# A one-layer streaming-encoder trunk on one core: a conditioning row loaded once and spread by products with ones, and the short chunks of the second feed-forward product put first

## The chip, the cores and the metric

The kernel runs on one core of one Trainium2 chip. The metric is device time in microseconds (us) of one execution; lower is better. The time before the change is the median of three executions, 2311.63 us (2308.95 to 2312.49).

## What is computed

One layer, 512 tokens, width 2048, feed-forward width 5632, all in 32-bit floats. A conditioning vector `c` sets six modulation vectors; two head groups of eight heads each (a gated linear recurrence and a stick-breaking attention) share one input projection; a gated residual, a second modulated normalisation and a SwiGLU feed-forward net follow.

```python
cond = jax.nn.silu(c)                                    # c: (1, 2048)
mod = cond @ w_ada + b_ada                               # 6 x 2048
sh1, sc1, g1, sh2, sc2, g2 = split(mod, 6)
h = rms_norm(x, norm1_g) * (1.0 + sc1) + sh1
proj = h @ w_in
o = concat(hgrn2_mixer(proj[...]), stick_breaking_mixer(proj[...]))
x = x + g1 * (o @ w_out)
h = rms_norm(x, norm2_g) * (1.0 + sc2) + sh2
gate, up = split(h @ w_ffn_in, 2)                        # 5632 each
x = x + g2 * ((silu(gate) * up) @ w_ffn_out)
```

The change touches two ends of this: how `silu(c)` comes to stand in all 128 partitions, and the order in which the 44 blocks of 128 feed-forward rows go through the last product.

## The kernel before

Everything is written with a tile framework: the code names tiles and pools, and a list scheduler sets the order in which the instructions stand on each engine, from the order in the code, from priorities (`tc.high_priority`) and from its own estimate of when each operand is ready. Each engine then runs its own list strictly in that order. All loads and stores are issued by SyncE (SP), whose list is in order too; eight completion semaphores go round, so the ninth load waits until the first has landed.

Products run with both operands split in a rounded part and a rest (`split`, lines 212 to 222: ScalarE copies the rounded part, line 220, VectorE subtracts, line 221). Three matmuls of 512 columns then make one product of two tiles (high by high, high by rest, rest by high). Four buffers go round for the rounded parts, so a copy on ScalarE waits until TensorE has finished with the part split four places earlier.

**The start of the program** (lines 270 to 324, tile `st` in the profile). The host lays `c` out 128 times, so that `a["c"]` has 128 rows of 2048 numbers, 1 MB. Lines 274 to 278 load it in two halves, and the first modulation row of the weights `w_ada` (`ada_first`) in two halves between them; ScalarE applies silu to each half of `cond`. A modulation number is the sum along a row of `w_ada` times `cond`, one VectorE instruction with an accumulator (`gemv`, line 180). From the first two sums come `mod` (line 293) and `gain` (line 184), and with the gain ScalarE makes the first scaled and rounded tile of x, `hhi` (line 309), which the first matmul waits for; VectorE makes the rest, `hlo` (line 310). Between them stand the load of ScalarE's second activation table (line 279), a short exponential for the head groups (line 592), the split of the first weight tile `wi0` in two halves (lines 298 and 299), and the squares of x (lines 312 and 315). Then 16 steps of 24 matmuls follow, each with a row of `w_ada`, a weight tile and a block of x loaded for it.

**The second feed-forward product** (lines 1163 to 1283, tiles `foA`, `foB`, `foC`). A one-level Strassen scheme with seven products makes out of 44 blocks of 128 rows, paired into 22, and 512 tokens the 2048 output columns. The 22 pairs go in six chunks, `CHUNKS = (4, 4, 4, 4, 3, 3)`; each chunk is done for two column groups, which makes 12 units. In a unit the seven products stand in the order `ORDER`; a product of a chunk of n pairs is 6n matmuls, so a unit is 168 matmuls with n = 4 and 126 with n = 3. `multiply` (line 1174) splits the weights of a product two pairs at a time (instructions on 1024 columns; a third pair alone makes one of 512), and before it VectorE makes the Strassen sums of the weights (lines 1181 and 1245). `onto` (line 1193) takes a finished product out of PSUM: in the first chunk ScalarE copies it to the output tile `O` (line 1196), in later chunks ScalarE copies it to a quarter of `cond` (line 1201) and VectorE adds it (line 1202); two products per unit are added from PSUM directly (lines 1259 and 1266). This part of a unit does not depend on n. In the last chunk the finished output blocks are transposed by TensorE (tile `foB` with `ident`), scaled and added to the residual by VectorE (line 1213) and stored (line 1215), as far as they are ready, three after each product.

The left operands of the second product are made in the first one: `keep` (line 1056) turns each pair of finished feed-forward blocks into seven forms, splits them and stores them in DRAM tiles `opd`, one for each chunk (`parts`, line 1076, ScalarE's cast on line 1082, VectorE's on 1083); `load_op` (line 1018) brings them back into a ring of eleven places, a chunk ahead. For the last pair, at line 1081, the rounded parts go to the tile `cond`. Its sums and casts stand, by the schedule, in the middle of the first unit of the second product.

Of the kernel before, what the change touches and what calls it, by code (L numbers as in the profile page):

```python
# [14 lines left out]
AF = mybir.ActivationFunctionType  # L15
# [5 lines left out]
T = 512  # L21
# [2 lines left out]
FM = 44  # L24
HT = 256
HALF = 8
CHUNKS = (4, 4, 4, 4, 3, 3)
ORDER = (2, 1, 7, 6, 4, 5, 3)
AHEAD = 300
SC2_EARLY = 8  # L30
# [99 lines left out]
def trunk(ctx, tc, a):  # L130
    nc = tc.nc
    V, S, G = nc.vector, nc.scalar, nc.gpsimd
    clock = Clock()
    PE = Timed(nc.tensor, clock)
# [9 lines left out]
    def acc(name):  # L144
        return psum.tile([P, T], F32, tag="acc", name=name)

    def att(name):
        return psum.tile([P, T], F32, tag="att", name=name, bufs=2)
# [4 lines left out]
    cond = const.tile([P, D], F32, name="cond")  # L153
    small = const.tile([P, N_SMALL], F32, name="small")
    ones = const.tile([P, P], F32, name="ones")
# [15 lines left out]
    def raw_tile(shape, name):  # L171
        return wp.tile(shape, F32, tag="raw", name=name, bufs=4)
# [97 lines left out]
    banks = [acc(f"st{i}") for i in range(4)] + [att(f"st{i + 4}") for i in range(2)]  # L270
    wide = att2("st6")
    banks += [wide[:, 0:T], wide[:, T:2 * T]]
    r0 = raw_tile([P, D], "ada_first")
    for i in range(2):
        sl = slice(i * 1024, i * 1024 + 1024)
        nc.sync.dma_start(cond[:, sl], a["c"][:, sl])
        nc.sync.dma_start(r0[:, sl], a["w_ada"][SC1 * KT][:, sl])
        S.activation(cond[:, sl], cond[:, sl], AF.Silu)
    tc.keep_in_program_order(S.preload_act_table_set("natural_log_exp_and_others"))
    nc.sync.dma_start(small, a["small"])  # L280
    w0 = raw_tile([P, 1024], "wi0r")
# [4 lines left out]
    for k in range(KT):  # L286
        xk = xo[:, k]
        if k == 0:
            for i in range(2):
                sl = slice(i * 1024, i * 1024 + 1024)  # L290
# [704 lines left out]
    rp = tctx.enter_context(tc.tile_pool(name="rp", bufs=1, side="right", reuse_waits="tile"))  # L995
    opd = [dram.tile([P, 7, n, 2 * HT], F32, name=f"opd{c}") for c, n in enumerate(CHUNKS)]
    starts = [sum(CHUNKS[:c]) for c in range(len(CHUNKS))]

# [11 lines left out]

    units = [(c, i) for c in range(len(CHUNKS)) for i in range(2)]
    places, blocks = [], [{} for _ in units]

    def place(n):
        n %= 11
        return places[0][:, n] if n < 4 else places[1][:, n - 4] if n < 7 else places[2][:, n - 7]

    def load_op(c, q):
        if c < len(CHUNKS):
            nc.sync.dma_start(place(7 * c + q)[:, 0:CHUNKS[c]].bitcast(F32),  # L1020
                              opd[c][:, ORDER[q] - 1].rearrange("p n (h t) -> p n h t", h=2))

    def load_y(u, b):
        if u == len(units):
            return
        c, i = units[u]
        n = CHUNKS[c]
        t = raw_tile([P, n, T], f"wfo{u}_{b}") if b % 2 == 0 else yraw[u > 0][:, b // 2, 0:n]
# [314 lines left out]
```

## Time and profile before

| | |
|---|---|
| median of three executions | 2311.63 us (2308.95 to 2312.49) |
| the profiled execution's own time | 2309.45 us |
| its span, first to last instruction | 2307.6 us |
| granted TensorE clock, mean | 0.995 |
| busy: TensorE matmuls, VectorE, ScalarE | 98%, 83%, 50% |
| DMA rate over the span | 190 GB/s; 368 GB/s in the first fortieth |
| stages by TensorE's tile: first projection `st` | from 11.54 us |
| second feed-forward product `fo` | from 1850.33 us |

The profile is one execution. A row of the timeline gives start, duration, engine, line, operation and operands (out<-in); in square brackets stands the time for which the engine was idle before it and what ended the wait. Matmuls are pipelined: the recorded 0.39 us of one overlaps with the next, and the distance of the starts is what TensorE needs. A row of the windows gives the busy time and number of instructions of each engine in a stretch of time, then the granted TensorE clock (PEclk), the DMA share and rate.

### The profile page before, as it was taken

Reading aid. Unit: us, or ns where it says so; the run is one execution under the profiler, and the core shown is the slowest. Engines: PE = TensorE matmul, PEld = TensorE weight load, DVE = VectorE, ACT = ScalarE, POOL = GpSimd, SP = SyncE. Lnnn points to the kernel's source line nnn. Section 1 sums busy time; section 2 is a strip of 40 time slices with the busy share of each in tenths; the row PEclk is TensorE's granted clock in tenths of the full one; section 3 lists DMA queues with packets and bytes.
Section 4 is the critical chain, followed back from the end, with each engine's and each line's share of the span. In section 5 each row is a group of like instructions: output and inputs, shape, how many; then the busy total and the mean of one; then the engine's idle time right before and its main releaser. Section 6 shows DMA issues by size and latency. Waiting matters only on the chain.

```text
span 2307.6 us, 35720 instructions
## 1 busy us (share of the span) xinstructions
PE 2253.1 (98%) x14171; PEld 2049.8 (89%) x14171; DVE 1919.5 (83%) x2570; ACT 1160.1 (50%) x2011; POOL 10.7 (0%) x25
## 2 busy tenths in 40 slices
PE   8999899999999999989999999999999999999998
PEld 6899799888888788989999999999999978878776
DVE  8887779999887864699899988888888777888888
ACT  4326666565656422654445444454545545454443
POOL 0000000000000000000000000000000000000000
PEclk9999999999999999999999999999999999999999
DMA  9886446843322486336555534454544486654553
GB/s 368 314 319 225 166 153 230 305 170 126 110 92 76 155 294 209 111 114 238 206 203 197 209 133 165 142 174 142 174 142 157 177 343 237 219 178 142 183 204 87
DMA packets 114978, 437.69 MB, mean 190 GB/s; under 512 B 9822, under 2 KB 58236, under 8 KB 76796
## 3 DMA queue, kind: packets, MB, share of 16 engines
q1 hardware_dynamic: 114812, 435.42, 53.0%
q8 instruction: 111, 1.82, 0.3%
q14 instruction: 55, 0.45, 0.1%
HBM read 386.61 MB, written 48.77 MB: 189 GB/s over the span
## 4 chain that ended last, share of the span: by engine, by line
PE 79%; DVE 11%; DMA 4%; ACT 3%; issue 3%; SPq 0%; DVEq 0%; ACTq 0%
PE ffA L93 17%; PE ffC L93 9%; PE foA L93 8%; PE sbp L93 8%; PE wo L93 7%; PE ffB L93 4%; PE foC L93 4%; PE st L93 4%; PE hgf L93 4%; PE hgq L93 3%; PE hgg L93 3%; PE foB L93 1%; DVE ada L180 1%; PE l L93 1%; DMA opd<-fhi 1%
## 5 line engine op out<-in xcount | busy, mean ns | idle before, releaser
L180 DVE SCALAR_TENSOR_TENSOR ada<-ada,cond 128x2048 f32<-128x2048 f32 x95 | 216.9, 2286 | 49.0 <-DMA ada<-in_w_ada 49.0
L93 PE MATMUL ffA<-opD,ff_3h 128*128 128x256 f32 x512 | 93.6, 283 | 0.8 <-ACT u L1008 0.8
L93 PE MATMUL ffA<-opB,ff_6h 128*128 128x256 f32 x512 | 93.6, 283 | 0.2 <-ACT a L1008 0.2
L93 PE MATMUL ffC<-opB,ff_7h 128*128 128x256 f32 x512 | 93.5, 283 | 0.0
L93 PE MATMUL ffC<-opC,ff_4h 128*128 128x256 f32 x496 | 90.8, 284 | 0.4 <-ACT c L1008 0.3
L93 PE MATMUL ffB<-opA,ff_2h 128*128 128x256 f32 x496 | 91.3, 284 | 0.0
L93 PE MATMUL ffA<-opC,ff_5h 128*128 128x256 f32 x496 | 90.6, 283 | 0.0
L93 PE MATMUL ffA<-opA,ff_1h 128*128 128x256 f32 x496 | 90.6, 283 | 0.0
L1082 ACT CAST fhi<-forms 128x512 fp32r<-128x512 f32 (+1 forms) x63 | 43.6, 692 | 90.6 <-DMA opd<-fhi 74.1
L93 PEld LDWEIGHTS ffA<-opD,ff_3h 128*128 128x128 f32 x512 | 79.8, 192 | 1.0 <-ACT u L1008 1.0
L93 PEld LDWEIGHTS ffA<-opB,ff_6h 128*128 128x128 f32 x512 | 79.7, 192 | 0.4 <-ACT a L1008 0.4
L93 PEld LDWEIGHTS ffC<-opB,ff_7h 128*128 128x128 f32 x512 | 79.8, 192 | 0.0
L93 PEld LDWEIGHTS ffC<-opC,ff_4h 128*128 128x128 f32 x496 | 77.2, 192 | 0.8 <-ACT c L1008 0.8
L93 PEld LDWEIGHTS ffB<-opA,ff_2h 128*128 128x128 f32 x496 | 77.7, 193 | 0.1
L93 PEld LDWEIGHTS ffA<-opC,ff_5h 128*128 128x128 f32 x496 | 77.3, 192 | 0.0
L93 PEld LDWEIGHTS ffA<-opA,ff_1h 128*128 128x128 f32 x496 | 77.3, 192 | 0.0
L1083 DVE TENSOR_TENSOR forms<-forms,fhi 128x512 fp32r<-128x512 f32 (+1 forms) x63 | 49.0, 778 | 31.0 <-ACT fhi L1082 30.6
L93 PE MATMUL ffA<-opD,ff_3l 128*128 128x256 f32 x256 | 72.5, 283 | 0.0
L93 PE MATMUL ffC<-opB,ff_7l 128*128 128x256 f32 x256 | 72.4, 283 | 0.0
L93 PE MATMUL ffA<-opB,ff_6l 128*128 128x256 f32 x256 | 72.4, 283 | 0.0
L93 PE MATMUL ffB<-opA,ff_2l 128*128 128x256 f32 x248 | 70.3, 284 | 0.0
L93 PE MATMUL ffA<-opA,ff_1l 128*128 128x256 f32 x248 | 70.2, 283 | 0.0
(1644 smaller groups left out, 7759.3 us busy)
## 6 DMA issues: line engine op xcount, KB each, us to landing
ada<-in_w_ada SPq DMA_DIRECT2D x95, 1024.0 KB, 5.0
wfo<-in_w_fo SPq DMA_DIRECT2D x16, 1024.0 KB, 6.0
yraw<-in_w_fo SPq DMA_DIRECT2D x16, 1024.0 KB, 5.1
fix<-in_w_fix SPq DMA_DIRECT2D x14, 1024.0 KB, 5.7
opsA<-opd SPq DMA_DIRECT2D x12, 1024.0 KB, 4.9
opd<-forms SPq DMA_DIRECT2D x44, 256.0 KB, 3.7
opd<-fhi SPq DMA_DIRECT2D x42, 256.0 KB, 4.2
opd<-forms SPq DMA_DIRECT2D x22, 384.0 KB, 6.7
```

The lines of the kernel that those rows point to most:

```text
L93: self.engine.matmul(out, lhsT, rhs, **kw)
L180: V.scalar_tensor_tensor(w, w, 1.0, row, op0=ALU.mult, op1=ALU.mult, accum_out=col)
L1082: S.copy(hi, R[:, q])
L1083: V.tensor_sub(R[:, q].bitcast(F32R), R[:, q], hi.bitcast(F32))
```

## The change

There are two independent parts. The first loads one row of `c` (8 KB) instead of 128; for each quarter of 512 columns a matmul with a row of ones as the stationary operand copies the row into all 128 partitions of a PSUM tile, and ScalarE applies silu from there into `cond`. The load of the row goes ahead of both halves of `ada_first`. The second part turns the chunk sizes round. Lines after 282 move down by four.

```diff
-CHUNKS = (4, 4, 4, 4, 3, 3)
+CHUNKS = (3, 3, 4, 4, 4, 4)
...
     r0 = raw_tile([P, D], "ada_first")
+    nc.sync.dma_start(cond[0:1], a["c"][0:1])
     for i in range(2):
         sl = slice(i * 1024, i * 1024 + 1024)
-        nc.sync.dma_start(cond[:, sl], a["c"][:, sl])
         nc.sync.dma_start(r0[:, sl], a["w_ada"][SC1 * KT][:, sl])
-        S.activation(cond[:, sl], cond[:, sl], AF.Silu)
+
+    for i in range(4):
+        sl = slice(i * T, i * T + T)
+        PE.matmul(banks[4 + i], ones[0:1], cond[0:1, sl], start=True, stop=True)
+        S.activation(cond[:, sl], banks[4 + i], AF.Silu)
```

The schedule moves with both parts. At the start of the program, on ScalarE, the list before begins like this (`st_...` are PSUM tiles, `wi0` the first weight tile, `xo` blocks of x; in brackets what the instruction waits for, DMAHW being a load):

```order
L278 ACT_TABLE_LOAD
L278 ACTIVATE cond<-cond 128x1024 [waits DMAHW0_49]
L278 ACTIVATE cond<-cond 128x1024 [waits DMAHW2_49]
L279 ACT_TABLE_LOAD
L298 CAST wi0h<-wi0r 128x512 [waits DMAHW5_49]
L592 ACTIVATE lbt<-lbt 128x8 [waits DVE_49]
L309 ACTIVATE hhi<-xo,gain_80 128x512 [waits DMAHW6_49,DVE_49]
```

After the change the same list begins so:

```order
L282 ACT_TABLE_LOAD [waits DMAHW0_49]
L282 ACTIVATE cond<-st_102 128x512 [waits PE_49]
L282 ACTIVATE cond<-st_103 128x512 [waits PE_49]
L302 CAST wi0h<-wi0r 128x512 [waits DMAHW4_49]
L282 ACTIVATE cond<-st_104 128x512 [waits PE_49]
L316 ACTIVATE ss_97<-xo 128x512 [waits DMAHW5_49]
L302 CAST wi0h<-wi0r 128x512 [waits DMAHW6_49]
L319 ACTIVATE sq_174<-xo 128x512 [waits DMAHW7_49]
L282 ACTIVATE cond<-st_104 128x512 [waits PE_49]
L283 ACT_TABLE_LOAD
L596 ACTIVATE lbt<-lbt 128x8 [waits DVE_49]
L313 ACTIVATE hhi<-xo,gain_80 128x512 [waits DVE_49]
```

The third silu has moved behind the cast of the first half of `wi0`, and the fourth behind both casts and the squares of two blocks of x. VectorE's list at the same place reads before:

```order
L180 SCALAR_TENSOR_TENSOR ada_first,lead<-ada_first,cond 128x1024 x2
L517 TENSOR_SCALAR qkg<-small 128x1
L518 COPY qkg<-small 128x1
L293 SCALAR_TENSOR_TENSOR mod<-lead,small 128x1
L591 TENSOR_TENSOR lbt<-small 128x8
L184 SCALAR_TENSOR_TENSOR gain_80<-mod,small 128x1
L299 TENSOR_TENSOR wi0l<-wi0r,wi0h 128x512
L594 RECIPROCAL lbs<-lbt 128x8
L595 TENSOR_TENSOR lbt<-lbt,lbs 128x8
L310 SCALAR_TENSOR_TENSOR hlo<-xo,gain_80,hhi 128x512
```

and after:

```order
L599 TENSOR_TENSOR lbt<-lbt,lbs 128x8
L184 SCALAR_TENSOR_TENSOR gain_80<-mod,small 128x1
L600 TENSOR_TENSOR lbt<-lbt 128x8
L601 TENSOR_SCALAR oml<-lbt 128x8
L180 SCALAR_TENSOR_TENSOR ada_161,mod<-ada_161,cond 128x2048
L314 SCALAR_TENSOR_TENSOR hlo<-xo,gain_80,hhi 128x512
```

These rows come after the two `ada_first` sums, between which now stand the rests of `wi0` and the first sum of squares; the reciprocal of `lbt` stands ahead of `mod` and `gain`, and the first `hlo` stands behind the next row's sum of 2048 columns.

In the first unit of the second product, on ScalarE, the list before is (`wfo_4_2h` is the second split of that unit's fifth product, `forms` holds the last feed-forward pair, `O` the output):

```order
L220 CAST wfo_4_0h<-wfo_2_18705 128x1024 [waits DVE_49,PE_49,Activation_49]
L220 CAST wfo_4_2h<-wfo_2_18705 128x1024 [waits DVE_49,PE_49,Activation_49]
L1082 CAST cond<-forms_18478 128x512 [waits DVE_49]
L1082 CAST cond<-forms_18478 128x768 [waits DVE_49]
L1082 CAST cond<-forms_18478 128x512
L1196 COPY O<-foA_18745 128x512 [waits DMAHW5_49]
L1196 COPY O<-foA_18746 128x512
L1196 COPY O<-foC 128x512 x2
```

After the change it is:

```order
L220 CAST wfo_4_0h<-wfo_2_18710 128x1024 [waits DVE_49,PE_49,Activation_49]
L1086 CAST cond<-forms_18483 128x512 [waits DVE_49]
L220 CAST wfo_4_2h<-wfo_2_18710 128x512 [waits PE_49,Activation_49]
L1086 CAST cond<-forms_18483 128x512 [waits DVE_49]
L1086 CAST cond<-forms_18483 128x768 [waits DVE_49]
L1200 COPY O<-foA_18750 128x512 [waits DMAHW4_49]
L1200 COPY O<-foA_18751 128x512
L1200 COPY O<-foC 128x512 x2
```

One of the three casts of the last pair has moved ahead of the split `wfo_4_2h`, the split has half its columns, and the copies to `O` still stand behind all of them.

On TensorE, in some units the third product (`foC`) begins in the middle of the second (`foA`). Of the units with three pairs the tenth is such a one before the change:

```order
L93 MATMUL foA0_18745<-wfo9_1_2h_21035,opsC_18998 128x512
L93 MATMUL foA0_18745<-wfo9_1_2l_21036,opsC_18998 128x512
L93 MATMUL foA0_18745<-wfo9_1_2h_21035,opsC_18998 128x512
L93 MATMUL foC_18751<-opsB_18715,opsC_18998 128x512 x12
L93 MATMUL foC_18751<-wfo9_2_2h_21068,opsC_18998 128x512
```

After the change it is the fourth unit:

```order
L93 MATMUL foA0_18750<-wfo3_1_2h_19429,opsC_18961 128x512
L93 MATMUL foA0_18750<-wfo3_1_2l_19430,opsC_18961 128x512
L93 MATMUL foA0_18750<-wfo3_1_2h_19429,opsC_18961 128x512
L93 MATMUL foC_18756<-opsB_18720,opsC_18961 128x512 x12
L93 MATMUL foC_18756<-wfo3_2_2h_19462,opsC_18961 128x512
```

What stood in the tenth unit stands in the fourth; in the first three units the second product stands whole, before and after.

## The prediction

> **What bounds the kernel now.** I read the page's first lines, then who TensorE waits for, then the chain that ended last, then the timeline of the two places that the change touches.
>
> ```profile
> span 2307.6 us, 35720 instructions
> PE 2253.1 (98%) x14171; PEld 2049.8 (89%) x14171; DVE 1919.5 (83%) x2570; ACT 1160.1 (50%) x2011; POOL 10.7 (0%) x25
> ```
>
> ```profile
> PE st L93 <- ACT hhi L309: 11.5, 1, 11.5
> PE foA L93 <- ACT O L1196: 3.4, 1, 3.4
> ```
>
> ```profile
> 11.54 88.72 PE st L93 x378
> ```
>
> TensorE is the bound: busy 98% of the span. Its longest waits are the 11.5 us until the first matmul and, third in that view, 3.4 us in the first unit of the second product; the change touches both places. From the first matmul on, the chain runs through TensorE without a break for 88.72 us, so whatever delays that matmul delays all that follows, and what makes a transfer shorter helps only if the first matmul comes sooner. The profiled execution took 2309.45 us, 1.85 around its span and 2.2 under the median of three, 2311.63; I add the changes to the median. A measurement of this kernel can tell about 0.2%, 4.6 us, from no change.
>
> **Part one, the conditioning row.** The start of the program, with the loads' medians below it:
>
> ```profile
> 0.74 0.40 SPq L276 DMA_DIRECT2D cond<-in_c  x1
> 4.64 1.06 ACT L278 ACTIVATE cond<-cond 128x1024 f32<-128x1024 f32 x1 [2.63 <-DMA cond<-in_c]
> 5.97 1.23 DVE L180 SCALAR_TENSOR_TENSOR ada_first<-ada_first,cond 128x1024 f32<-128x1024 f32 x1 [5.97 <-DMA ada_first<-in_w_ada]
> 8.74 1.28 ACT L279 ACT_TABLE_LOAD   x1
> 9.04 1.23 DVE L180 SCALAR_TENSOR_TENSOR ada_first<-ada_first,cond 128x1024 f32<-128x1024 f32 x1 [1.84 <-DMA ada_first<-in_w_ada]
> 10.03 0.62 ACT L298 CAST wi0h<-wi0r 128x512 fp32r<-128x512 f32 x1
> 10.57 0.16 DVE L184 SCALAR_TENSOR_TENSOR gain<-mod,small 128x1 f32<-128x1 f32 x1
> 10.64 0.21 ACT L592 ACTIVATE lbt<-lbt 128x8 f32<-128x8 f32 x1
> 11.54 0.80 PE L93 MATMUL st<-wi0h,hhi 128*128 128x512 f32 x1 [11.54 <-ACT hhi L309]
> 11.61 0.75 DVE L310 SCALAR_TENSOR_TENSOR hlo<-xo,gain,hhi 128x512 fp32r<-128x512 f32 x1
> 11.91 0.60 ACT L298 CAST wi0h<-wi0r 128x512 fp32r<-128x512 f32 x1
> 12.42 0.62 ACT L315 ACTIVATE sq<-xo 128x512 f32<-128x512 f32 x1
> 14.38 2.29 DVE L180 SCALAR_TENSOR_TENSOR ada<-ada,cond 128x2048 f32<-128x2048 f32 x1 [0.54 <-DMA ada<-in_w_ada]
> ```
>
> ```profile
> cond<-in_c SPq DMA_DIRECT2D x2, 512.0 KB, 3.9
> out_y<-O SPq DMA_DIRECT2D x32, 128.0 KB, 1.9
> ```
>
> Now the loads set the pace here: the second sum waits until 9.04 for its weights. Both halves of `cond` gone, what is queued behind them lands up to 3.07 us sooner (9.04 less 5.97, one half of each). That would be a gain, if the order on ScalarE stayed. It doesn't: the fourth silu, without which the second sum can't run, now stands behind two casts and two squares, and ahead of the table load.
>
> The four products with ones come first on TensorE. Their price is that of the one product of this form in the trace, the sum of squares:
>
> ```profile
> 101.97 1.02 PE L93 MATMUL ssum<-ss,ones 128*128 128x512 f32 x2
> 103.00 0.34 PE L93 MATMUL sbp<-wsb_0l,hhi 128*128 128x384 f32 x1
> 103.17 0.34 PE L93 MATMUL sbp<-wsb_0h,hlo 128*128 128x384 f32 x1
> ```
>
> From 101.97 to 103.00 it and one matmul of 384 columns were done; the latter takes 0.17 (103.00 to 103.17), so the product takes 0.86. At the start TensorE is at half pace:
>
> ```profile
> 13.98:17.39 3.41, 3.41 (x10) 1.00 1.04 422
> 17.39:20.80 3.41, 3.41 (x17) 1.00 1.03 405
> 1867.42:1870.83 3.41, 0.56 (x2) 1.00 0.20 67
> 1870.83:1874.24 3.41, 3.41 (x9) 0.50 0.93 308
> ```
>
> In equal stretches there are 10 matmuls before 17.39 us and 17 after it; the column of the granted clock has no record for the start, but at 1870.83, after 2.85 us of idleness in one stretch of 3.41, it says 0.50 for the next, with the same 9 or 10. So a product with ones takes 1.72 at the start.
>
> The sum, from the row's load at 0.74: landed 2.6 (1.9 later, as the 128 KB of `out_y`, the nearest in size; 3.9 as `cond` is the other bound), three products 5.2, so 7.8; the third silu 0.6 (a 512-column activation, as the cast at 10.03), 8.4; squares 0.62, cast 0.60, squares 0.62, 10.2; the fourth silu, 10.8. The loads they need are there: even the second block of x, in place by 12.42 before, has landed by 9.4. The fourth product, which waits for the third silu, is done by 10.1. Then the second sum 1.23 on VectorE, beside the table load 1.28 and the exponential 0.21 on ScalarE, to 12.3; the reciprocal, `mod` and `lbt` ahead of `gain`, about 0.2 each as the rows of this size: `gain` at 12.9. From `gain` to the first matmul 0.97, as now (10.57 to 11.54): 13.87, less about 0.1 for each pair of overlapping ScalarE instructions (11.91 to 12.42 is 0.51 for 0.60): 13.6. That is 2.1 later than 11.54. Then `hlo`, which the sixth matmul needs, stands behind a sum of 2.29: it is done 0.3 + 2.29 + 0.75 after `gain`, near 16.2, while five matmuls at half pace (0.34 apart at 10 in 3.41, up to 0.43 by twice the later pace) end at 15.3 to 15.8: 0.4 to 0.9 of waiting, 0.5 taken. The half pace lasted from 11.54 to 17.39, 5.85; stretches of 3.41 that do not start with the program would make it 3.4 to 6.8, 5.1 on the mean; half of the difference of 0.75 is 0.3 to gain. Sum of part one: **+2.3**. Bounds: if the row lands after 3.9, +4.3; if the first three products run at full pace, the first cast, whose load can land no sooner than about 7.0, takes their place, and I find +1.5. A gain is excluded only as long as ScalarE's order holds.
>
> The Trainium skill, "ScalarE: Activation LUTs", section "What ACT_TABLE_LOAD costs", gives 1.28 us for the load of a table and 1.38 for a drain behind it, 2.66 in all. Here the load of 8.74 is followed by a cast at 10.03, so this trace shows the 1.28 alone; by the page part one would be 1.4 dearer.
>
> **Part two, the short chunks first.** The units of the second product, from first matmul to first matmul (first, second, fourth, and the last four):
>
> ```profile
> 1850.33:1893.79 43.46, 40.03 (x171) 32.60 (x169) 32.07 (x34) 21.36 (x27) 0.00 (x0) 0.96 0.90 356
> 1893.79:1931.87 38.08, 38.08 (x170) 31.53 (x168) 28.46 (x27) 19.79 (x24) 0.00 (x0) 1.00 0.79 303
> 1969.95:2009.59 39.64, 39.00 (x169) 31.30 (x168) 33.17 (x35) 18.73 (x22) 0.00 (x0) 1.00 0.72 265
> 2168.19:2198.87 30.68, 30.24 (x129) 23.61 (x128) 25.70 (x34) 15.21 (x22) 0.00 (x0) 1.00 0.40 129
> 2198.87:2230.89 32.02, 30.10 (x128) 23.33 (x126) 26.78 (x35) 15.08 (x22) 0.00 (x0) 1.00 0.66 228
> 2230.89:2264.42 33.53, 31.73 (x144) 24.74 (x142) 31.32 (x45) 15.24 (x23) 0.00 (x0) 1.00 0.45 147
> 2264.42:2299.15 34.73, 32.97 (x157) 26.04 (x156) 32.45 (x50) 12.91 (x19) 0.00 (x0) 1.00 0.22 61
> ```
>
> The second unit has no stall: 168 matmuls in 38.08, 0.2267 each; 126 would take 28.56. A unit of four pairs once the additions have begun takes 39.64, so it loses 1.56. Those of three pairs lose more, since VectorE is at 26.78 in 32.02 (84%) and taking products out of PSUM costs it the same for a smaller unit: the tenth loses 32.02 - 28.56 = 3.46, the ninth (128 matmuls fall in its stretch, 29.02) 1.66. The last two, with the output's transposes, take 68.26 for 250 matmuls (56.7): 11.6 over. The first loses 5.38: the wait of 3.4 and one stretch of half clock, 1.7. All losses: 5.38 + 5 x 1.56 + 1.66 + 3.46 + 11.6 = 29.9.
>
> After the change the first unit has this to it:
>
> ```profile
> 1864.89 0.68 DVE L1064 TENSOR_TENSOR forms<-sg,up 128x512 f32<-128x512 f32 x1
> 1866.92 1.04 ACT L220 CAST wfo_2h<-wfo 128x1024 fp32r<-128x1024 f32 x1 [1.67 <-PE foC L93]
> 1867.88 1.87 ACT L1082 CAST cond<-forms 128x512 fp32r<-128x512 f32 x3
> 1869.65 1.06 ACT L1196 COPY O<-foA 128x512 f32<-128x512 f32 x2
> ```
>
> The copies that TensorE's fourth product waits for stand behind a split that waits for the end of the third product, and behind the casts of the last pair. The third product ends at 1866.8 now and three quarters as far in after the change, 1862.7. With it the split moves; and VectorE, whose list from 1848.73 to `forms` at 1864.89 is back to back (16.2 us for 14 instructions of 1024 columns), has seven of the 14 cut to 512, 0.55 less each, and gets there some 3.9 sooner, at 1861. The copies follow 3.4 after the product, one cast being ahead (0.5 less) and the split shorter (0.5 less), but the last sums being 1 later: the wait stays at 3.4, and the half clock with it, 5.3. The second unit has nothing to add in either version: 0. The third has its second product whole, as before, where it lost nothing: 0 (at most the ninth's 1.66). The fourth stands as the tenth did: 3.46. Units five to ten are of four pairs: 6 x 1.56 = 9.36. The last two: 11.6 less what a unit of four loses less than one of three, 1.9 (3.46 - 1.56) for one of them, not both, as VectorE then also has the outputs: 9.7. Sum 27.8, so part two gives **-2.1**. Bounds: -4.8 if the fourth loses 1.66 and the last two gain 0.9 more; +1.2 if the second and third lose as the ninth did.
>
> Work on TensorE is the same otherwise (four products more, in the wait), and the loads scale with the units. Both parts: +2.3 - 2.1 = +0.2, on the median **2311.8**; against the profiled execution 2309.65.
>
> **The rivals.**
>
> *The short first unit does not cover its fixed chain* (slower). If the copies to `O` still start at 1869.65 because `forms` or a buffer comes no sooner, TensorE stands at 1862.8 and waits 7.5 instead of 3.4, +4.1, and a second stretch falls to half clock, +1.7: 2311.8 + 5.8 = 2317.6. It decides once the copies start 2.5 us later than I have them, at 1867.9. For it: the casts of the last pair are of fixed size. Against it: VectorE's list ahead of them is mostly work that shrinks. 0.15.
>
> *The products with ones release the clock.* They keep TensorE busy for 5 to 7 us at half pace; if that makes full pace last until the real matmuls, the 2.9 us lost to half pace (5.85 / 2) fall away, while the wait for `hlo` grows by 0.9: 2311.8 - 1.7 (0.3 was in the sum) = 2310.1. Against it: from the fourth product's end at 10.1 TensorE is idle for 3.5 us, and 2.85 in one stretch sufficed at 1867. 0.15. The Trainium skill, "TensorE: Matmul & The Clock Gate", section "Why this matters for your kernels", advises 4 us of matmuls as a warm-up; its section "What's actually happening" has a window of 3.4 us without work undo it, as the windows above show.
>
> *The lighter loads carry the start after all* (faster): the silus are not late, because the waits on ScalarE end sooner than I have them, and the first matmul comes 2.6 to 3.07 earlier: -2.6 - 2.1 = 2306.9. For it: 9.04 is a wait for a load. Against it: ScalarE's order. 0.10.
>
> **How the numbers follow.** The forecast, 0.60, gives 2311.8 and by its bounds (+1.5 - 4.8 to +4.3 + 1.2, on the median) some 2308.3 to 2317.1; with the scatter of a measurement its ends count 0.02 for faster and 0.03 for slower. Faster by over 0.2%, under 2307.0: the third rival in half its cases, the forecast's end and 0.01 of the second rival, 0.08. Slower, over 2316.3: most of the first rival, 0.12, and the forecast's end, 0.15 in all. The same: 0.77. The range takes in the second rival and most of the first: 2307.5 to 2317.6.
>
> **What would show it.** Right: the first matmul of `st` (not of the ones) near 13.6, waiting for `hhi`; the fourth silu near 10.2; the first unit 28.6 + 5.3 long with a wait for `O` of about 3.4; the second and third units near 28.6, the fourth near 32, the next six near 39.6. Wrong: a first matmul before 11.5 or after 15; a wait for `O` over 6; stalls of 3 in the second or third unit; or losses of over 2.5 in the units of four pairs, where the chunk sizes do not matter by my account.

## The result, and the profile after

After the change the kernel takes 2313.90 us (median of 20 executions, 2310.01 to 2316.91); before, on the same chips, 2310.89 (20 executions, 2305.73 to 2313.65). The ratio is 1.0016, 95% interval 1.0009 to 1.0022: slower by 3.0 us by the medians and by 3.7 by the ratio, which is clear of no difference but less than the 0.2%, 4.6 us, that the prediction set as its bound (the interval reaches 0.22%). The forecast was 0.2 us slower, on a median of 2311.63. The time is inside the range of 2307.5 to 2317.6; its two terms are looked at below, because one of them came out twice as large as forecast.

The page of the profile after, its first lines, and the waits of TensorE (engine, line and releaser; in all, times, longest):

```profile
span 2313.0 us, 35739 instructions
PE 2262.2 (98%) x14179; PEld 2053.0 (89%) x14179; DVE 1918.7 (83%) x2570; ACT 1159.6 (50%) x2013; POOL 10.7 (0%) x25
```

```profile
PE st L93 <- ACT hhi L313: 3.5, 1, 3.5
PE sbo L93 <- ACT L L468: 3.4, 3, 2.0
PE foA L93 <- ACT O L1200: 3.4, 1, 3.4
```

The first row looks like a wait of 11.5 that became one of 3.5. It isn't: TensorE now does the products with ones in the same stretch, and the first matmul of `st` comes later than before. The timeline of the start after the change:

```profile
2.59 5.45 PE L93 MATMUL st<-cond,ones 1*128 1x512 f32 x6 [2.59 <-DMA cond<-in_c]
4.66 0.60 ACT L282 ACTIVATE cond<-st 128x512 f32<-128x512 f32 x1 [0.86 <-PE st L93]
6.37 0.60 ACT L282 ACTIVATE cond<-st 128x512 f32<-128x512 f32 x1 [1.11 <-PE st L93]
7.84 0.62 ACT L302 CAST wi0h<-wi0r 128x512 fp32r<-128x512 f32 x1 [0.88 <-DMA wi0r<-in_w_hi]
8.37 0.59 ACT L282 ACTIVATE cond<-st 128x512 f32<-128x512 f32 x1
9.01 2.07 PE L93 MATMUL st<-cond,ones 1*128 1x512 f32 x2 [0.97 <-ACT cond L282]
9.88 0.63 ACT L319 ACTIVATE sq<-xo 128x512 f32<-128x512 f32 x1
11.11 0.60 ACT L282 ACTIVATE cond<-st 128x512 f32<-128x512 f32 x1 [0.60 <-PE st L93]
11.74 1.23 DVE L180 SCALAR_TENSOR_TENSOR ada_first<-ada_first,cond 128x1024 f32<-128x1024 f32 x1 [0.43 <-ACT cond L282]
13.59 0.16 DVE L184 SCALAR_TENSOR_TENSOR gain<-mod,small 128x1 f32<-128x1 f32 x1
14.56 0.79 PE L93 MATMUL st<-wi0h,hhi 128*128 128x512 f32 x1 [3.48 <-ACT hhi L313]
```

Each product is recorded as two matmuls. Three stand back to back; the fourth waits 0.97 us for the third silu, though it has nothing to do with it, and the fourth silu waits for the fourth product: ScalarE is through with the casts and squares ahead of it at 10.51 and idles for 0.60 us. The first matmul of `st` is at 14.56 against 11.54: 3.0 later.

The units of the second product after the change (first, second, fourth, fifth, sixth, and the last two together, to the last transpose):

```profile
1858.91:1891.74 32.83, 29.45 (x131) 23.80 (x129) 24.46 (x33) 17.57 (x27) 0.00 (x0) 1.00 0.84 325
1891.74:1920.40 28.66, 28.66 (x127) 23.50 (x126) 22.13 (x27) 16.06 (x25) 0.00 (x0) 1.00 0.84 310
1949.08:1981.10 32.02, 30.10 (x128) 23.33 (x126) 27.32 (x35) 15.53 (x22) 0.00 (x0) 1.00 0.72 266
1981.10:2021.64 40.54, 38.48 (x168) 30.77 (x166) 34.08 (x36) 18.84 (x22) 0.00 (x0) 1.00 0.48 179
2021.64:2061.26 39.62, 38.95 (x169) 31.31 (x168) 33.17 (x35) 18.73 (x22) 0.00 (x0) 1.00 0.72 266
2219.87:2309.02 89.15, 86.97 (x401) 68.45 (x399) 78.33 (x102) 34.48 (x41) 0.00 (x0) 1.00 0.25 76
```

The whole second product, from its first matmul to the last transpose, before and after, and the last two units of before:

```profile
1850.33:2303.51 453.18, 439.53 (x1914) 351.54 (x1912) 378.31 (x431) 211.99 (x269) 0.00 (x0) 1.00 0.56 197
1858.91:2309.02 450.11, 437.39 (x1914) 349.71 (x1912) 378.11 (x431) 212.12 (x269) 0.00 (x0) 1.00 0.55 199
2230.89:2303.51 72.62, 68.00 (x315) 52.61 (x313) 67.86 (x103) 28.15 (x41) 0.00 (x0) 1.00 0.34 104
```

It takes 450.1 us, against 453.2 before: 3.1 shorter. But it begins 8.6 later than before, at 1858.91 against 1850.33. Of that, 3.0 is the start; the rest was added on the way, and a part of it belongs to this one execution. The averages of four traces with the start as before (before, and e2, e7, e10 below) and of four with the changed start (after, e1, e9, e12) show how the lag, the time by which the changed start comes later to the same matmul, grows and shrinks:

| TensorE reaches | old start, us | changed start, us | lag |
|---|---|---|---|
| first matmul of `st` | 11.6 | 14.5 | +2.9 |
| second round of `sbp` | 137.3 | 139.2 | +1.9 |
| first `hgg` | 464.3 | 467.3 | +3.0 |
| last `wo` | 941.4 | 945.5 | +4.1 |
| second feed-forward product | 1851.6 | 1856.2 | +4.6 |

Up to the last `wo` the two groups stand apart (there 940.7 to 942.2 us against 944.0 to 946.8). In the last row they overlap (1849.8 to 1855.6 against 1853.2 to 1858.9), so its lag is uncertain by some 2 us.

### The profile page after: what moved, and what is told of

Read it like the earlier page. It is cut to its first block, busy times and chain, and to the rows that moved or that the text cites. A ratio compares the mean times of both kernels' runs of the same rounds, so it can differ in the third digit from the quotient of the medians.

```text
span 2313.0 us, 35739 instructions
## 1 busy us (share of the span) xinstructions
PE 2262.2 (98%) x14179; PEld 2053.0 (89%) x14179; DVE 1918.7 (83%) x2570; ACT 1159.6 (50%) x2013; POOL 10.7 (0%) x25
## 4 chain that ended last, share of the span: by engine, by line
PE 71%; DVE 16%; DMA 5%; issue 4%; ACT 4%; SPq 0%; DVEq 0%; ACTq 0%
PE ffA L93 16%; PE foA L93 8%; PE ffC L93 8%; PE wo L93 7%; PE sbp L93 6%; PE ffB L93 4%; PE st L93 4%; PE foC L93 4%; PE hgf L93 4%; PE hgq L93 3%; PE hgg L93 3%; DMA opd<-fhi 2%; DMA ada<-in_w_ada 1%; DVE wfo_2l L221 1%; DVE yraw L1185 1%
## 5 line engine op out<-in xcount | busy, mean ns | idle before, releaser
L93 PE MATMUL ffA<-opC,ff_5l 128*128 128x256 f32 x248 | 70.2, 283 | 0.0
```

What stands on the lines that cost most here:

```text
L93: self.engine.matmul(out, lhsT, rhs, **kw)
```

## The experiments

State of the theories before them: A, the row's part costs more than forecast because the fourth product waits, and the chunks bring about what was forecast; B, the whole lag of the start passes to the end and the chunks are worth nothing; C, the chunks make the kernel slower.

**e1 and e2: each part alone.**

```diff
e1: the changed kernel with
-CHUNKS = (3, 3, 4, 4, 4, 4)
+CHUNKS = (4, 4, 4, 4, 3, 3)
e2: the kernel before with
-CHUNKS = (4, 4, 4, 4, 3, 3)
+CHUNKS = (3, 3, 4, 4, 4, 4)
```

> The row and its products, the chunks as before the change. In the trace after the change the first matmul of st came at 14.55 us (3.0 later than before) and the fourth silu at 11.11, and by 140 us the lag was down to 1.8, since TensorE no longer waited there for a weight tile. Theory A (the start is what the change pays, part of it is given back): first matmul 14.5, lag 1.5 to 2.2 at 140 us, median 1.5 to 3 above before. Theory B (the whole lag passes to the end): 3 to 3.5 above. Theory C (the slower time comes from the chunks): within 1 of before.

> The short chunks first, the conditioning row as before. In the trace after the change the stretch from the first matmul of the second product to the end was 454.1 us against 457.3. Theory A (the chunks bring what that stretch shows, less what the clock's chance gave, 1.7): 1.5 to 3.2 under before. Theory B (the gain is the chance of one execution, the fifth unit gives back what the last two gain): within 1 of before. Theory C: above before by 1 or more. In the trace: first unit with a wait for O near 3.5, second and third units near 28.7, fourth near 32, fifth 1 to 1.5 longer than the ones behind it.

Measured: e1 2315.99 us (11 executions), ratio to before 1.0020 (1.0011 to 1.0029), 4.6 slower; e2 2309.05 (11), ratio 0.9990 (0.9981 to 0.9998), 2.4 faster; before 2311.42. C falls, and B's half on the chunks. By the median the row costs more than A gave it (1.5 to 3) and more than the lag of the start, though the interval, 2.5 to 6.7 us, takes in A's upper end and B's 3 to 3.5; what adds to the lag on the way is the question of e6 and e9. In e2 the units stand as forecast, and its first unit shows the half clock that the one after the change was spared:

```profile
1855.59:1890.03 34.44, 31.07 (x131) 24.93 (x129) 24.44 (x33) 17.56 (x27) 0.00 (x0) 0.95 0.82 314
1868.70:1872.11 3.41, 0.72 (x3) 0.64 (x4) 3.36 (x6) 2.74 (x6) 0.00 (x0) 1.00 0.32 108
1872.11:1875.53 3.42, 3.42 (x10) 2.64 (x9) 0.00 (x0) 0.69 (x2) 0.00 (x0) 0.51 1.01 329
```

In the traces of e3, e4, e5, e6, e8 and e9, which have the same chunks, half clock follows that wait too; the profile after the change is the exception.

**e3 and e5: the PSUM tile or the order on ScalarE.** The third and fourth product go to the two halves of one PSUM tile (`wide`). e3 gives each a tile of its own; e5 leaves the tiles and puts the casts, squares and the exponential behind the last silu.

```diff
e3: the changed kernel with
-        PE.matmul(banks[4 + i], ones[0:1], cond[0:1, sl], start=True, stop=True)
-        S.activation(cond[:, sl], banks[4 + i], AF.Silu)
+        PE.matmul(banks[i], ones[0:1], cond[0:1, sl], start=True, stop=True)
+        S.activation(cond[:, sl], banks[i], AF.Silu)
e5: the changed kernel with
-        S.activation(cond[:, sl], banks[4 + i], AF.Silu)
+        silu = S.activation(cond[:, sl], banks[4 + i], AF.Silu)
...
-                S.copy(whi[:, sl], w0[:, sl])
+                with tc.issue_after(silu.ins):
+                    S.copy(whi[:, sl], w0[:, sl])
...
```

> Both parts of the change, but the four products with ones go into four PSUM tiles of their own, where the third and the fourth shared one tile. Theory A (the fourth product waited for the third silu because of the shared tile, and the schedule put the fourth silu late because of it): the fourth product starts near 7.8 instead of 9.0, the fourth silu near 9.9 instead of 11.1, the first matmul of st near 13.0 instead of 14.55; median 0.7 to 1.5 under the changed kernel. Rival (the order on ScalarE, casts and squares, is what makes it late, whatever the tile): the fourth silu still at 10.8 or later, first matmul at 14 or later.

> Both parts of the change and its PSUM tiles, but on ScalarE the four silus stand ahead of the casts of wi0, the squares of x and the exponential. Theory A (the shared PSUM tile and the products' price set the fourth silu; the order adds little): the third silu near 8.1, the fourth product near 8.8, the fourth silu near 10.8 (11.1 in the changed kernel), and as both casts now come behind it, the first matmul of st near 14.5 again; median within 1.5 of the changed kernel. Rival (the order on ScalarE is what the start costs, as the prediction had it): fourth silu under 10.2, first matmul under 14. At 331 us, where all three kernels with one load fewer at the start stood 1.3 to 1.8 us longer than those with the old number of loads: the same long wait of 2.3.

e3's four products run without a gap, and the first matmul comes at 12.99, as theory A had it:

```profile
2.58 7.16 PE L93 MATMUL st<-cond,ones 1*128 1x512 f32 x8 [2.58 <-DMA cond<-in_c]
9.78 0.60 ACT L282 ACTIVATE cond<-st 128x512 f32<-128x512 f32 x1 [0.35 <-PE st L93]
12.99 0.79 PE L93 MATMUL st<-wi0h,hhi 128*128 128x512 f32 x1 [3.24 <-ACT hhi L313]
```

In e5 the third silu is at 8.19, yet the fourth product still waits for it, and the fourth silu is at 10.95:

```profile
8.84 2.07 PE L93 MATMUL st<-cond,ones 1*128 1x512 f32 x2 [0.69 <-ACT cond L282]
10.95 0.60 ACT L282 ACTIVATE cond<-st 128x512 f32<-128x512 f32 x1 [2.16 <-PE st L93]
14.67 0.79 PE L93 MATMUL st<-wi0h,hhi 128*128 128x512 f32 x1 [3.76 <-ACT hhi L314]
```

So the shared tile set the fourth silu: without it the silu comes 1.3 us sooner (e3), with it the other order on ScalarE brings 0.2 (e5). The 1.3 are not the tile's alone, though. In e3 the schedule also put the second cast and the second squares behind the fourth silu; in the changed kernel they end at 10.51, so with their order kept the tile could give back 0.6 (11.11 to 10.51), and the other 0.7 needs both. Medians: e3 2314.26 (11), ratio 1.0009 (0.9999 to 1.0018); e5 2315.32 (8), ratio 1.0024 (1.0015 to 1.0034). e3 recovers 1.6 of the start's lag; in time it is 0.4 over the changed kernel by the medians and 1.6 under by the ratios, so the 0.7 to 1.5 that were expected of it are neither confirmed nor excluded.

**e4 and e8: half of the row.** The first 1024 columns are loaded in 128 rows as before, the second 1024 are spread by two products; in e4 the 512 KB load goes first, in e8 the 4 KB one. The rest of the edit, not shown here, puts the exponential of `lbt` and the second cast of `wi0` behind the first scaled tile. For e4:

```diff
+    nc.sync.dma_start(cond[:, 0:1024], a["c"][:, 0:1024])
+    nc.sync.dma_start(cond[0:1, 1024:D], a["c"][0:1, 1024:D])
...
+    S.activation(cond[:, 0:1024], cond[:, 0:1024], AF.Silu)
+    for i in range(2):
+        PE.matmul(banks[6 + i], ones[0:1], cond[0:1, 1024 + i * T:1024 + i * T + T], start=True, stop=True)
+    S.activation(cond[:, 1024:D], wide, AF.Silu)
...
```

> Both parts of the change, but only the second half of the row is spread by (two) products, into one PSUM tile with one silu behind them; the first half is loaded in 128 rows as before the change. On ScalarE the exponential of lbt and the second cast of wi0 are put behind the first scaled tile. Theory A (the price of the start is in the four products at half pace, 1.7 each, and in the order on ScalarE; the lighter load is worth what the row of before says): second sum at 7.5 instead of 9.0 before, first matmul of st near 10.3, 1.2 before that of the kernel before. Of this TensorE gives some back near 137 us, where it waits for a weight tile. Median 1 to 4 under the changed kernel. Rival (the loads behind are no sooner, since all 16 transfer engines are shared): second sum at 8.5 or later, first matmul at 11.3 or later.

> As e4, but the 4 KB of the row's second half are loaded ahead of the 512 KB of the first half. In e4 they landed at 4.0 us, behind that load, and the silu of the second half came at 7.8. Theory A: products from 2.5 to 6.0, second sum near 8.4, first matmul of st near 10.8 (11.4 in e4), and more than half of this gain gone by 140 us, where TensorE waits for a weight tile; median within 1 of e4. Rival (the gain passes to the end): 0.6 under e4 or more, and more than 2.5 under the kernel before.

```profile
4.01 3.75 PE L93 MATMUL st<-cond,ones 1*128 1x512 f32 x4 [4.01 <-DMA cond<-in_c]
11.42 0.79 PE L93 MATMUL st<-wi0h,hhi 128*128 128x512 f32 x1 [3.67 <-ACT hhi L312]
```

In e4 the 4 KB landed at 4.01, behind the 512 KB, and the first matmul came at 11.42, not 10.3: the expectation failed on that, and the rival's numbers held (second sum at 8.85, first matmul at 11.3 or later). e8 put it right: products from 2.35, first matmul at 10.82 as expected. Medians: e4 2309.83 (11), ratio 0.9991 (0.9981 to 1.0001); e8 2312.51 (11), ratio 1.0005 (0.9994 to 1.0015). Both have the chunks that alone brought 2.4, so an earlier first matmul brought nothing that can be measured; e8 was expected within 1 of e4, and is 2.7 over it by the medians, for a reason that the runs don't show. The two profiles differ by 5.0 us of span, with e8 the longer. In the trace's clock records e8 has 34 us at half clock behind its start and ahead of the last 5 us, e4 24, which could be worth 5. But 3.6 of the difference arose between the last `wo` and the second product (912.6 us in e8, 909.0 in e4), where both have 6.8 us at half clock, so the clock is not the whole of it.

**e6 and e9: one load fewer.** The changed kernel issues one load less at the start. Eight completion semaphores go round, so every later load uses the neighbour of the one it had before. e6 loads the row in two halves; e9 leaves the start alone and loads the identity, at the end of the first projection, in two halves.

```diff
e9: the changed kernel with
-                nc.sync.dma_start(ident2, a["cst"][:, 0])
+                for h in (slice(0, 64), slice(64, P)):
+                    nc.sync.dma_start(ident2[:, h], a["cst"][:, 0, h])
```

> Both parts of the change, but the row is loaded in two halves of 4 KB, so that the program has as many loads as before the change, and every later load gets back the completion semaphore that it had before. The schedule then also has the four silus first. Theory L (one load fewer moves all later loads to the neighbouring semaphore and ring, and that makes loads land later near 310 to 322 us): the wait for L at 331 us is back to 0.5 to 1.0 instead of 2.3, median 1 to 2 under e5. Rival (the lag of the start itself makes that wait): the wait at 331 stays 2.3. First matmul of st near 14.1 by either.

> The changed kernel as it is, with one edit far behind its start: the identity that is loaded at the end of the first projection comes in two halves, so that from there on every load has the completion semaphore that it had before the change; the order on ScalarE, VectorE and TensorE is the same but for one sum and one copy near 100 us. The first mask load lands 3.67 to 3.86 us after its issue in the six traces with the old numbering and 4.28 to 4.51 in the four with the new one. Theory L (the numbering alone makes that): 3.7 to 3.9 here, the wait for L at 331 us down from 2.3 to about 1.5, median about 1 under the changed kernel. Rival (the lag of the start, 3.0, makes it): 4.3 or more, wait 2.3, same median.

The load of the mask and a broadcast near 310 us (KB, us to landing), and the TensorE wait behind them, before:

```profile
mskr<-in_msk SPq DMA_DIRECT2D x1, 512.0 KB, 3.7
xo<-drow SPq DMA_DIRECT2D x1, 256.0 KB, 4.5
330.67 1.16 PE L93 MATMUL sbo<-scr,L 128*128 128x128 f32 x8 [0.53 <-ACT L L464]
```

after the change:

```profile
mskr<-in_msk SPq DMA_DIRECT2D x1, 512.0 KB, 4.5
xo<-drow SPq DMA_DIRECT2D x1, 256.0 KB, 5.6
334.15 1.16 PE L93 MATMUL sbo<-scr,L 128*128 128x128 f32 x8 [1.96 <-ACT L L468]
```

and in e9:

```profile
mskr<-in_msk SPq DMA_DIRECT2D x1, 512.0 KB, 3.9
xo<-drow SPq DMA_DIRECT2D x1, 256.0 KB, 5.8
333.95 1.16 PE L93 MATMUL sbo<-scr,L 128*128 128x128 f32 x8 [1.39 <-ACT L L469]
```

(The expectations count this wait from start to start of the matmuls: 2.3 where the row has 1.96 of idleness.) With the old numbering the mask lands in 3.67 to 3.86 us in nine traces, e6 and e9 among them; with the new one in 4.28 to 4.57 in five. The wait itself falls into three groups: 0.5 to 0.7 us of idleness in the seven traces without the four products, 1.2 and 1.4 in e6 and e9, which have the four products and the old numbering, and 1.8 to 2.1 in the five that have the four products and the new one. So the numbering makes some 0.6 of it (0.57 between e9 and after); whether by the semaphore or by something else that goes round with the count of loads, no run tells. The other part goes with the broadcast `xo<-drow`, which lands in 4.4 to 4.5 us in the seven traces without the four products (the old start and that of e4, e8 and e11), and in 5.6 to 6.0 in the seven with the whole row spread, whatever the numbering; why, is not settled. Medians: e6 2314.88 (10), ratio 1.0022 (1.0012 to 1.0032), first matmul at 13.76; e9 2313.83 (12), ratio 1.0012 (1.0002 to 1.0022). So theory L holds for the mask's load. It does not hold in full for the wait, which from start to start is 1.55 in e6 (0.5 to 1.0 expected) and 1.73 in e9 (about 1.5); and its 0.6 us do not show in the time: e6 is 0.4 under e5 where 1 to 2 were expected, and e9 level with the changed kernel where about 1 was.

**e7 and e10: a chunk of two, first or last**, on the kernel before.

```diff
e7:
-CHUNKS = (4, 4, 4, 4, 3, 3)
+CHUNKS = (2, 4, 4, 4, 4, 4)
e10:
-CHUNKS = (4, 4, 4, 4, 3, 3)
+CHUNKS = (4, 4, 4, 4, 4, 2)
```

> The conditioning row as before the change; chunks of (2, 4, 4, 4, 4, 4) pairs, so that no chunk of three is left and the two units with nothing to add have half the matmuls. Theory A (units with additions lose what VectorE's fixed part costs, 1.56 with four pairs and up to 3.5 with three): first unit 19.0 and 3 to 5 over, second near 19.1, third to tenth near 39.6 each, last two together near 84; 1 to 3 under the median of e2, 2306 to 2308. Rival (a first unit of two pairs is too short for its fixed chain, the casts of the last pair and the copies to O): wait for O over 6, and the median not under that of e2.

> The conditioning row as before the change; chunks of (4, 4, 4, 4, 4, 2): the sizes of e7 with the chunk of two last instead of first. Theory A (a unit with additions needs VectorE for a fixed part whatever its size, so a short chunk is free only where nothing is added): the last two units take near 56 us for 168 matmuls (38.1), 18 over, and the first and second stay as before; median 3 to 6 over before, 2314 to 2317. Rival (what counts is that two odd chunks of three, with a split of one pair by itself, are gone, wherever the chunk of two stands): median 2301 to 2306.

e7 takes 2302.09 us (5 executions, 2301.08 to 2304.01), ratio to before 0.9969 (0.9957 to 0.9981): 8.6 us under the 2310.71 of before in the same comparison (7.2 by the ratio), and the fastest kernel of this study. That is 4 us below the 2306 to 2308 that theory A gave. Its first four units, and the last two to the last transpose:

```profile
1850.58:1871.94 21.36, 19.41 (x87) 15.70 (x85) 18.07 (x22) 13.94 (x20) 0.00 (x0) 1.00 0.94 349
1871.94:1890.98 19.04, 19.04 (x86) 15.77 (x84) 14.78 (x15) 13.28 (x18) 0.00 (x0) 1.00 1.01 421
1890.98:1929.06 38.08, 38.08 (x170) 31.53 (x168) 32.38 (x34) 19.19 (x23) 0.00 (x0) 1.00 0.73 280
1929.06:1968.74 39.68, 39.09 (x170) 31.22 (x168) 33.18 (x35) 18.72 (x22) 0.00 (x0) 1.00 0.73 260
2206.66:2295.76 89.10, 87.26 (x401) 68.53 (x399) 78.07 (x102) 34.48 (x41) 0.00 (x0) 1.00 0.25 77
```

The first unit loses 2.3 (the wait for `O` is 2.0, and no half clock follows), the second and third nothing, and the fourth to tenth 1.6 each. From the first matmul to the last transpose it is 445.2 us against 453.2. Of these 8.0 the first unit brings 3.1 (5.4 lost before), the last two 3.0 (15.9 before, 12.9 here), and the two units of three pairs that are gone 1.9. The expectation had given the first unit 3 to 5 of loss.

e10, the same sizes in the other order: 2309.78 us (12), ratio 0.9994 (0.9983 to 1.0006), not to be told from before, and 5.8 over e7 by the ratios, 7.7 by the medians; from the first matmul to the last transpose it takes 452.9 us, 7.7 more than e7. Its last two units, of two pairs:

```profile
2246.94:2302.72 55.78, 49.57 (x233) 38.47 (x231) 52.32 (x80) 21.10 (x28) 0.00 (x0) 0.95 0.37 107
```

55.8 for work of 38.1, 18 over, as theory A said; VectorE is busy for 52.32 of them. The time expected, 2314 to 2317, did not come, since the sum made of it was wrong: 11.6 had been taken for the last two units of before, which ends at the last product. To the last transpose, as here, they lose 15.9, so e10 gives back only 1.8 there and gains as much in the units of three that are gone. The rival (position does not matter) falls.

**e11 and e12: the row with the chunks of e7.** e11 has e4's start, e12 the changed one, both with `CHUNKS = (2, 4, 4, 4, 4, 4)`.

> The start of e4 (first half of the row in 128 rows, second half by two products) with the chunks of e7. First matmul near 11.4 us as in e4 and in the kernel before. Theory A (e4's start is worth nothing that lasts, its time was that of the chunks): within 1 of e7, 2301 to 2303.5. Rival (an earlier end of the half pace, some 1.4 us in e4, lasts): 2299 to 2301.

> The row and its four products as the change has them, with the chunks of e7; the row's price against a second background. e1 against the kernel before showed 4.6 (2.5 to 6.7), the changed kernel against e2 some 4 to 5. Theory A (start 3.0 later, 1.2 of it given back by 140 us, 1.5 added at 331 us by loads that land later, some more in the half-clock stretches): 3 to 5 over e7, 2305 to 2307. Rival (the start alone, without anything added: 1.5 to 2.5): 2303.5 to 2304.5.

e11 2303.98 us (11), ratio 0.9970 (0.9959 to 0.9981); e12 2306.68 (12), ratio 0.9982 (0.9973 to 0.9990). By the ratios, and 2311 us for before, e12 is 3.0 over e7, e11 0.2; by the medians 4.6 and 1.9. e12 is where theory A had it, e11 0.5 above its range. The first matmul of e11's profiled execution was at 12.8, not at 11.4, because its first sum had its weights at 8.62 and not at 7.04 as in e4; one trace does not say how often that happens. The row costs 4.6 against the kernel before, 3.0 by the ratios or 4.6 by the medians against e7, and 6.0 or 4.9 against e2 (the changed kernel has the same chunks): 3 to 6 us, and none of the other starts that were tried measurably beats the one of the kernel before.

## Why the prediction was right, and where it was not

**The time.** It lies 2.1 us above the forecast of 2311.8, and the difference to the kernel before is too small for the bound, as forecast. The two parts have the signs that were forecast, +2.3 and -2.1; they measured +4.6 (2.5 to 6.7) and -2.4 (-4.4 to -0.5). Added up these are +2.2, against 3.0 to 3.7 for both together, a difference that the intervals cover. The error of the whole is the row's, 2.3 of some 3 us. It is the width of the range that kept the time inside it; that the two terms all but cancel, which the forecast rested on, did not come true.

**Part one, the step that failed.** The row landed and the first three products took what the sum has: first product at 2.59 (2.6), 5.45 for three (1.72 each, 5.2). Then two steps are off. "The fourth product, which waits for the third silu, is done by 10.1" was added up as 8.4 for the silu's end and 1.72 for the product. But the third silu ended at 8.96: it stands behind the first cast, which got its weights only at 7.84, a wait that the sum does not have. And from the product's start at 9.01 to the fourth silu's it took 2.1, not 1.72. So the product was done at 11.1, behind the casts and squares (10.51) instead of ahead of them, and the fourth silu began at 11.11, not at 10.2: of this 0.9, ScalarE's list makes 0.3 and the wait for the product 0.6. The first matmul came at 14.56 instead of 13.6 by it, nearer to the 15 that the prediction gave as a sign of being wrong. The rest of this sum stands: `gain` to first matmul 0.97, and half pace until 19.79, 5.2 after the first matmul (5.1 forecast); only the wait for `hlo` was smaller, 0.13 by the starts of the matmuls (16.43 to 16.99, where 0.43 is the pace), with 0.5 forecast.

The second error is the sentence "whatever delays that matmul delays all that follows". Of a lag of 2.9 TensorE has 1.9 left at 137 us, since it waits there for a weight tile whose load does not come later by as much:

```profile
137.53 0.62 PE L93 MATMUL sbp<-wsb_0h,hhi 128*128 128x384 f32 x2 [1.33 <-ACT wsb_0h L220]
139.38 0.62 PE L93 MATMUL sbp<-wsb_0h,hhi 128*128 128x384 f32 x2 [0.26 <-ACT wsb_0h L220]
```

(before, and after). And 1.1 to 1.4 come back at 331 (1.9 to 3.0 in the table; 0.53 to 1.96 in the rows above), where the mask and the broadcast, which e6 and e9 looked at, land later. Both lie outside the two places that the prediction looked at. The last 1.1 to 1.6 come up to the end of `wo` and behind it. At the start of `wo` a pause of 2.8 us in two parts, which every trace has (2.7 to 3.1), fell on two of the 3.41 us stretches before:

```profile
764.91:768.32 3.41, 2.10 (x14) 1.65 (x12) 3.08 (x6) 2.85 (x6) 0.00 (x0) 1.00 0.13 55
768.32:771.73 3.41, 1.88 (x9) 1.33 (x8) 3.41 (x7) 3.41 (x8) 0.00 (x0) 1.00 0.70 221
```

and mostly on one after the change:

```profile
770.72:774.13 3.41, 0.87 (x3) 0.44 (x4) 3.41 (x5) 3.41 (x7) 0.00 (x0) 1.00 0.23 60
774.13:777.55 3.42, 3.42 (x9) 2.64 (x10) 3.42 (x7) 3.42 (x8) 0.00 (x0) 0.50 0.59 247
```

with half clock behind it, 1.7 us. It happened in two of the four traces with the changed start, in none of the four with the old one, and in all six with another start (e3, e4, e5, e6, e8, e11). In the executions that were not profiled the place cannot be seen, but the mean granted clock can: 0.9936 over the eleven of e1 and 0.9937 over the 33 of before, so that both lose some 14.6 us to half pace, alike to within about 0.7. So on the mean half pace does not explain the row's price. Behind `wo`, up to the second product, eight traces take 908.3 to 909.9 us and six 912.1 to 913.4 (after, e1, e2, e5, e8, e11), with the old start and with others; why is open, and so is whether the row costs anything beyond the lag of 3.0, which the interval of the 4.6 takes in.

**Part two.** The wait for `O` stayed at 3.4, as forecast (3.4); the half clock behind it came in seven of the eight traces with these chunks (e2: 34.44 for 29.0, 5.4 lost) and not in the changed kernel's profile (32.83, 3.8). Second and third unit 28.66 and 28.68 (28.6), fourth 32.02 (32). One term was missed: the fifth unit, the first of four pairs behind those of three, takes 40.54 for 166 matmuls and loses 2.9, 1.3 more than the 1.56 it was given; so it does in e2 and e3. A loss of over 2.5 in a unit of four pairs was a sign of being wrong, and it did show: the chunk sizes matter to the first unit of four pairs behind those of three (behind the two units of two pairs, in e7, the next one loses nothing). What makes this loss is open. The last two units lose 13.0 to the last transpose, against 15.9 before: 2.9 gained, 1.9 forecast. By the same measure before loses 34.2 in all, the changed kernel 31.2, e2 32.8: 1.5 to 3.1 gained, 2.1 forecast. Over all eight traces with these chunks the second product takes 450.1 to 453.1 us, 451.8 on the mean, and in the two with the old chunks and their order (before, e1) 453.2 and 454.0: 1.7 gained, so the size of part two was right, with an error on the fifth unit and one on the last two that all but cancel.

**The rivals.** The short first unit does cover its fixed chain: the copies to `O` start in time, and even two pairs leave a wait of only 2.0 (e7). The products with ones do not release the clock: in the seven traces with the four products, half pace ended 3.2 to 6.0 us behind the first real matmul, in the four with the old start 3.5 to 6.0. The lighter loads do not carry the start: the first sum waits for its silu at 7.00, not for the load. The draining 1.38 us behind a table load, of which the Trainium skill speaks ("ScalarE: Activation LUTs", section "What ACT_TABLE_LOAD costs"), is not to be seen here either: after the change the load of 11.73 lasts 1.28, and the exponential starts at 13.02.

## What to carry to other kernels

Ask of a short piece of work what its neighbours do for a fixed price beside it: a short chunk is free where nothing is added to an earlier result (e7), and dear where the additions or the output stand (e10); one chunk of two, put first, beats two of three (e7 is 4.9 us under e2 by the ratios). Whether that is because two is even, or because one short chunk is enough, no run separates. Where a small product is spread over halves of one tile, look for waits between the halves: they may share one dependency, as here, where a tile of its own brought up to 1.3 us at this place and nothing that could be measured in the time. And follow a shifted start through the next waits of the bottleneck before counting it in full; a part of it is swallowed by the first wait for something that does not move with it.

## What the runs showed of the hardware that was not expected

A pause of the same length, 2.7 to 3.1 us at the start of `wo`, cost nothing beyond itself (before, no half clock behind it), or 1.7 (after, 3.41 us at half clock), or 3.4 (e8 and e11, 6.83), depending on how it fell on stretches of 3.41 us of the clock's records. These do not start with the program: the first half pace ended at 17.39, 15.23, 17.45 and 17.50 us in the four traces with the same start. In all fourteen traces the share of a stretch at full clock in which TensorE was busy tells what follows: 76 of the 77 stretches with half clock behind them were busy for at most 0.51 (the other, 0.61, lies among the transposes at the end of e10), and of the 9205 others none for less than 0.44. From half clock, full clock came back behind stretches that were busy for 0.83 or more, 63 times, and did not behind 44 that were busy for 0.83 or less.

This makes a part of the scatter. Executions of the kernel before lie between 2305.7 and 2317.9 us, and those whose mean granted clock was 0.995 have a mean span of 2307.4 us (18 executions), those at 0.994 2309.1 (45) and those at 0.993 2310.1 (20). The 3 us that e1, e8 and e11 lose behind `wo` without any more half clock there than the faster traces show that there are other sources.

And a load of 512 KB landed 0.7 us later when one load fewer stood ahead of it, so that it used the neighbouring completion semaphore (3.67 to 3.86 us in nine traces, 4.28 to 4.57 in five); adding one small load ahead of it undid that.
